# One-hot rows of the expert gates kept with two tokens side by side instead of eight

## The chip, the cores and the metric

The kernel runs on one core of a Trainium2 chip. The metric is the device time of one execution in microseconds (us). The engines are TensorE (PE; its weight loads are listed apart as PEld), VectorE (DVE), ScalarE (ACT), GpSimd (POOL) and SyncE (SP). Each runs its own stream of instructions in order and waits on semaphores for the others.

## What is computed

A decoder block on 1024 tokens: a mixing part (RWKV-7 and differential attention), and then an expert network, in which each token picks 128 of 16,384 experts by two keys, `e1` and `e2`, of 128 values each. Only the expert part matters here:

```python
ids = (e1 * PK_NKEYS + e2).reshape(T, PK_HEADS * PK_TOPK)
gates = jax.nn.softmax(vals, axis=-1).reshape(T, PK_HEADS * PK_TOPK)
act = jnp.einsum('ced,cd->ce', u_tab[idc], xc)
act = jax.nn.gelu(act, approximate=False) * gc
return jnp.einsum('ce,ced->cd', act, v_tab[idc])
```

## The kernel before

The tokens lie in eight tiles of 128. The experts of the first four tiles are gathered: `peer` fetches one row of `u` or `v` per token and step through POOL (L809) into one of five `uv` buffers, and DVE takes the dot product (L831) or adds the scaled row (L838). The last four tiles go through `dense`, which multiplies their tokens with all 16,384 experts on PE and weighs each product by a gate matrix that is mostly zero. `gates` builds that matrix ahead of `dense`, one block of 128 tokens at a time, four blocks in all; `choose` (the selection of the experts, on DVE) runs ahead of each block and `ahead` (some products `ua` for `dense`) beside it.

In `gates`, `e1`, `e2` and the gate `g` lie with the 128 picks of a token down the partitions and the tokens along the row. For four tokens, DVE writes `oh`, a float32 one-hot row of `e1` per pick (L850, four buffers). For eight tokens, DVE writes `ohb`, a bfloat16 one-hot row of `e2` (L854, two buffers), in the order [key value][token]: the eight tokens stand side by side, so that one token's 128 values are eight elements, or 16 bytes, apart. For each token ACT copies that row, scaled by `g`, to the float32 tile `ohg` (L859, two buffers of four tokens), and PE multiplies `ohg` with `oh` into a PSUM bank `gb` (L860). When four tokens are done ACT evicts the bank to `st` (L861), and every 32 tokens a store of 2 MB takes `st` to DRAM (`gd_s`, L862), from where `dense` reads it back.

The comparison pattern for `ohb` is a constant `eye8` of 1024 values, each key value eight times in a row. It comes from DRAM as float32 (`eye_f`, 512 KB, L960) and DVE casts it to bfloat16 (L962), while `pick` still ranks keys.

The order of instructions on each engine is fixed when the program is built, by a scheduler that weighs estimated costs; so `ohb`, `oh`, the steps of `choose` and the dot products L831 stand in one given order on DVE, whatever the times on the chip are. The stores and loads that are named here go through SP's queue, the gathers through POOL's.

Of the kernel before, what the change touches and what calls it, by code (L numbers as in the profile page):

```python
# [8 lines left out]
F32 = mybir.dt.float32  # L9
F32R = mybir.dt.float32r  # L10
BF = mybir.dt.bfloat16
I32 = mybir.dt.int32
U32 = mybir.dt.uint32
AF = mybir.ActivationFunctionType
OP = mybir.AluOpType
# [3 lines left out]
P = 128  # L19
# [29 lines left out]
def body(ctx: ExitStack, tc: tile.TileContext, ins, out, dbg=None):  # L49
    nc = tc.nc  # L50
# [15 lines left out]
    def abank(name):  # L66
        return ps.tile([P, 512], F32, name=name, tag="ab", bufs=2)
# [53 lines left out]
    def const(name, shape, dt=F32):  # L121
        t = kp.tile(shape, dt, name=name)
        nc.sync.dma_start(t, ins[name])
        return t
# [17 lines left out]
    eye_row = const("eye_row", [P, P])  # L142
# [680 lines left out]
    def peer(bi, ids, gate):  # L823

        rows = slice(bi * P, (bi + 1) * P)
        act = pp_.tile([P, P], F32, name="act", bufs=2)
        hb = pp_.tile([P, D], F32, name="hb", tag="ha", bufs=2)
        nc.sync.dma_start(hb, ins["hfs"][rows, :])
        for j in range(P):
            u = gather("u", ids, j)  # L830
            nc.vector.scalar_tensor_tensor(u, u, 1.0, hb, op0=OP.mult, op1=OP.mult, accum_out=act[:, j:j + 1])  # L831
        nc.scalar.activation(act, act, AF.Gelu)
        nc.vector.tensor_tensor(act, act, gate, op=OP.mult)
        acc = pp_.tile([P, D], F32, name="acc", tag="ha", bufs=2)
        nc.sync.dma_start(acc, ins["x1s"][rows, :])
        for j in range(P):
            v = gather("v", ids, j)
            nc.vector.scalar_tensor_tensor(acc, v, act[:, j:j + 1], acc, op0=OP.mult, op1=OP.add)  # L838
        finish(acc, rows, pp_, "uv", NU)

    def gates(sp, a, sl, eye8):

        e1, g = sl[:, 0:P], sl[:, 2 * P:3 * P]
        e2 = sl[:, 3 * P:].bitcast(BF)[:, 0:P]
        nc.scalar.activation(e2, sl[:, P:2 * P], AF.Copy)
        for q in range(0, P, QT):
            st = sp.tile([P, P, QT], F32, name="st", bufs=2)
            for t in range(0, QT, 4):
                o1 = sp.tile([P, 4, P], F32, name="oh", bufs=4)
                nc.vector.tensor_tensor(o1, eye_row[:, None, :].to_broadcast([P, 4, P]),  # L850
                                        e1[:, q + t:q + t + 4, None].to_broadcast([P, 4, P]), op=OP.is_equal)
                if t % 8 == 0:
                    o2 = sp.tile([P, P, 8], BF, name="ohb", bufs=2)
                    nc.vector.tensor_tensor(o2, eye8, e2[:, None, q + t:q + t + 8].to_broadcast([P, P, 8]),  # L854
                                            op=OP.is_equal)
                b = abank("gb")
                o3 = sp.tile([P, 4, P], F32, name="ohg", bufs=2)
                for k in range(4):
                    nc.scalar.activation(o3[:, k], o2[:, :, t % 8 + k], AF.Copy, scale=g[:, q + t + k:q + t + k + 1])  # L859
                    nc.tensor.matmul(b[:, k:512:4], o3[:, k], o1[:, k], start=True, stop=True)  # L860
                nc.scalar.activation(st[:, :, t:t + 4], b.rearrange("p (e t) -> p e t", t=4), AF.Copy)  # L861
            nc.sync.dma_start(ins["gd_s"][:, :, (a * P + q) // QT].rearrange("c p f t -> p c (f t)"),  # L862
                              st.rearrange("p (c f) t -> p c (f t)", f=CE))
# [6 lines left out]
    def ahead(sp, W, fh, fl, es):  # L870

        for e in es:
            t = sp.tile([P, 512], F32, name="ue", bufs=2)[:, :W]
            nc.scalar.activation(t, dots(e, W, fh, fl), AF.Copy)
            nc.sync.dma_start(ins["a_s"][e, :, 0:W], t)
# [80 lines left out]
        late = pick(t0, W, fh, fl)  # L956
    if "nopeer" not in dbg:
        with tc.tile_pool(name="sp", bufs=1) as sp:
            eye_f = sp.tile([P, P * 8], F32, name="eye_f", bufs=1)
            nc.sync.dma_start(eye_f, ins["eye8"])  # L960
            eye8 = sp.tile([P, P, 8], BF, name="eye8", bufs=1)
            nc.vector.tensor_copy(eye8.rearrange("p e t -> p (e t)"), eye_f)  # L962
            o = W - ND * P
            fh, fl = fh[:, :, o:W], fl[:, :, o:W]
            for a, c in enumerate(late[o // P:]):
                gates(sp, a, choose(*c), eye8)
                ahead(sp, ND * P, fh, fl, range(a * NE // ND, (a + 1) * NE // ND))
            todo += [(c[2], *choose(*c)) for c in late[:o // P]]
        dense(t0 + o, ND * P, fh, fl)
        for t in todo:  # L970
            peer(*t)


def prepare(inputs):
    import numpy as np
    g = {k: np.asarray(v) for k, v in inputs.items()}
    c = np.ascontiguousarray
    f = np.float32
    a = {}
    a["x"] = c(g["x"].reshape(T, D))  # L980

    wt = lambda w: c(w.reshape(2, 4, P, -1, P).transpose(3, 0, 2, 1, 4).reshape(-1, 2, P, 512))
    a["w_in"] = wt(g["w_in"][0])
    a["proj"] = wt(np.concatenate([g["proj_a"][0], g["proj_b"][0]], axis=0))
    a["w_out"] = c(g["w_out"][0].reshape(8, P, 2, 512).transpose(0, 2, 1, 3))
    a["wq"] = wt(g["peer_wq"][0])
    a["keysT"] = c(g["peer_keys"][0].reshape(16, P, P).transpose(0, 2, 1))
    a["u"], a["v"] = c(g["peer_u"][0]), c(g["peer_v"][0])
    a["ut"] = c(a["u"].reshape(P, P, 2, 4, P).transpose(0, 2, 4, 3, 1).reshape(P, 2, P, 512))
    a["nmw"] = c(g["norm_mix_w"][0].reshape(1, D))  # L990
    a["nfw"] = c(g["norm_ffn_w"][0].reshape(1, D))
    a["fnw"] = c(g["final_norm_w"].reshape(1, D))
    col = lambda v, n: v.reshape(n, P).T
    a["pp"] = c(np.concatenate(
        [col(g["shift_mu"][0], 14)]
        + [col(g[n][0].reshape(-1), 4) for n in ("w0", "a0", "k_k", "k_a", "r_k", "lnx_w", "lnx_b")]
        + [g["subln_w"][0].reshape(P, 1)], axis=1))
    a["lam4"] = c(np.stack([g["lam_q1"][0], g["lam_q2"][0], g["lam_k1"][0], g["lam_k2"][0]], axis=1))
    a["lora"] = c(np.stack([np.concatenate([g["w2"][0], g["a2"][0]], axis=0), g["g2"][0]], axis=1))

    a["ident"] = np.eye(P, dtype=f)
    s = np.arange(P)[:, None] % CH
    t = np.arange(CH)[None, :]
    a["mask2"] = c(np.concatenate([t > s, t >= s], axis=1).astype(f))
    lv = []
    for b in (16, 32):
        lv.append(((s // (2 * b)) == (t // (2 * b))) & ((t // b) % 2 == 1) & ((s // b) % 2 == 0))
    a["lvl"] = c(np.stack(lv, axis=1).astype(f))
    a["eyec"] = (s == t).astype(f)
    p = np.arange(P)  # L1010
    same = (p[:, None] // CH) == (p[None, :] // CH)
    a["eye16"] = c(np.tile(np.eye(16, dtype=f)[None], (64, 1, 1)))
    a["blk"] = same.astype(f)
    rm = np.ones((P, 512), f)
    rm[:, ::CH] = 0
    a["rmask"] = rm
    dq = np.arange(P)[:, None] - (np.arange(T)[None, :] - 896)
    a["dist"] = np.where(dq >= 0, -dq, NEG).astype(f)
    a["eye_row"] = c(np.tile(np.arange(P, dtype=f)[None], (P, 1)))
    a["eye8"] = c(np.tile(np.repeat(np.arange(P, dtype=f), 8)[None], (P, 1)))  # L1020
    a["iota"] = c(np.tile(np.repeat(np.arange(16, dtype=f), 16)[None], (P, 1)))
    return a

# [23 lines left out]
```

## Time and profile before

| | us |
|---|---|
| median of 3 runs | 3443.16 (3440.47 to 3446.24) |
| the profiled execution, its own time | 3435.12 |
| its span, first to last instruction | 3433.4 |
| PE busy | 3041.2 (89%) |
| DVE busy | 2855.4 (83%) |
| ACT busy | 1410.6 (41%) |
| POOL busy | 1328.8 (39%) |
| `ohg`, L859 on ACT, 512 instructions | 228.5 busy, 1.8 idle ahead of them |

The mixing part and the ranking of keys run to about 1549 us, the four gate blocks from there to about 1871 us, and `dense` beside the gathers from there to the end. A busy share is an average over these stages. In what follows a stage is read by itself: busy time of each engine within a stretch, and who waits for whom in it. The granted clock of PE is a share of its full speed.

### The profile page before, as it was taken

The page shows a single profiled execution, that of the slowest core. Times are in us where ns is not written, and L with a number is a line of the kernel's source. Part 1 is how long each engine was busy: PE and PEld are TensorE (multiplying, and loading weights), DVE is VectorE, ACT ScalarE, POOL GpSimd, SP SyncE. Part 2 cuts the span into 40 slices and gives each one's busy share as a digit, 9 for nine tenths or more (in the row PEclk, how much of TensorE's full clock was granted, in tenths as well). Part 3 has the DMA queues.
Part 4 walks back from the last instruction along what each step waited for, and adds up shares of the span by engine and source line. Part 5 has one row for each costly group of instructions (what it writes and reads, how often), then busy time and mean ns, then how long its engine had stood idle before and what let it go on. Part 6 is the DMA issues. An engine that isn't in the chain of part 4 may idle for free.

```text
span 3433.4 us, 50842 instructions
## 1 busy us (share of the span) xinstructions
PE 3041.2 (89%) x17382; PEld 2379.3 (69%) x17382; DVE 2855.4 (83%) x6337; ACT 1410.6 (41%) x2632; POOL 1328.8 (39%) x1037
## 2 busy tenths in 40 slices
PE   7999998989988878798887689999998999898992
PEld 5777777766766656576565568777777777676872
DVE  5565548989898789998887689998989999889997
ACT  4444424434434423239998333333323333333331
POOL 0000000054533454212124256655655665655664
PEclk9999999999999889899988799999999999999996
DMA  4222444276666788656769999999999999999997
GB/s 135 81 77 74 140 152 161 81 253 209 216 217 222 274 322 314 204 164 187 234 202 324 333 321 353 362 348 353 355 365 350 359 354 355 360 358 350 350 327 275
DMA packets 407525, 898.68 MB, mean 262 GB/s; under 512 B 69025, under 2 KB 140001, under 8 KB 403169
## 3 DMA queue, kind: packets, MB, share of 16 engines
q0 software_dynamic: 147456, 536.94, 43.8%
q1 hardware_dynamic: 259808, 358.49, 31.2%
q8 instruction: 137, 2.24, 0.3%
q14 instruction: 124, 1.01, 0.1%
HBM read 829.22 MB, written 66.07 MB: 261 GB/s over the span
## 4 chain that ended last, share of the span: by engine, by line
issue 30%; PE 23%; POOL 18%; DVE 13%; DMA 13%; ACT 2%; POOLq 0%; SPq 0%; DVEq 0%; ACTq 0%
POOL uv L809 18%; DMA uv<-v,ids 9%; PE z L192 3%; PE z L196 3%; PE z L193 3%; DVE acc L838 2%; DMA uv<-u,ids 2%; DVE uv L831 2%; PE sc L544 1%; ACT ohg L859 1%; DVE wlo L178 1%; PE q L192 1%; PE q L196 1%; PE q L193 1%; PE oT L586 1%
## 5 line engine op out<-in xcount | busy, mean ns | idle before, releaser
L809 POOL DMA_INDIRECT uv<-u,ids x512 | 652.6, 1275 | 1226.5 <-DVE uv L831 639.4
L809 POOL DMA_INDIRECT uv<-v,ids x512 | 674.1, 1317 | 519.7 <-DVE acc L838 329.1
L838 DVE SCALAR_TENSOR_TENSOR acc<-uv,act,acc 128x1024 f32<-128x1024 f32 x512 | 655.9, 1281 | 75.7 <-DMA uv<-v,ids 70.1
L831 DVE SCALAR_TENSOR_TENSOR uv<-uv,hb 128x1024 f32<-128x1024 f32 x512 | 617.1, 1219 | 92.9 <-DMA uv<-u,ids 91.9
L177 ACT ACTIVATE whi<-wraw 128x512 fp32r<-128x512 f32 x552 | 339.8, 628 | 611.4 <-PE z L193 201.3
L178 DVE TENSOR_TENSOR wlo<-wraw,whi 128x512 fp32r<-128x512 f32 x552 | 375.0, 686 | 117.3 <-ACT whi L177 95.8
L192 PE MATMUL ua<-fh,whi 128*128 128x512 f32 x1024 | 415.9, 406 | 52.6 <-ACT ye L921 28.6
L193 PE MATMUL ua<-fl,whi 128*128 128x512 f32 x1024 | 413.3, 404 | 0.0
L199 ACT ACTIVATE ah<-gw 128x512 fp32r<-128x512 f32 x128 | 80.9, 632 | 682.4 <-DVE gw L901 682.4
L203 PE MATMUL yk<-vh,ah 128*128 128x512 f32 x768 | 308.5, 402 | 24.4 <-ACT ah L199 22.4
L205 PE MATMUL yk<-vh,al 128*128 128x512 f32 x768 | 308.4, 402 | 7.0 <-DVE al L200 6.7
L204 PE MATMUL yk<-vl,ah 128*128 128x512 f32 x768 | 304.3, 396 | 8.7 <-DVE vl L200 8.6
L196 PE MATMUL z<-hh,wlo 128*128 128x512 f32 x672 | 276.7, 412 | 6.0 <-DVE wlo L178 6.0
L192 PE MATMUL z<-hh,whi 128*128 128x512 f32 x672 | 276.6, 412 | 4.0 <-DVE carry L287 3.8
L196 PE MATMUL ua<-fh,wlo 128*128 128x512 f32 x1024 | 266.3, 398 | 15.3 <-DVE wlo L178 15.1
L193 PE MATMUL z<-hl,whi 128*128 128x512 f32 x672 | 274.6, 409 | 0.0
L192 PEld LDWEIGHTS ua<-fh,whi 128*128 128x128 f32 x1024 | 199.9, 195 | 100.2 <-ACT ye L921 32.1
L860 PE MATMUL gb<-oh,ohg 128*128 128x128 f32 x1024 | 226.4, 341 | 41.3 <-ACT ohg L859 40.4
L860 PEld LDWEIGHTS gb<-oh,ohg 128*128 128x128 f32 x1024 | 165.9, 209 | 105.2 <-ACT ohg L859 69.5
L196 PEld LDWEIGHTS ua<-fh,wlo 128*128 128x128 f32 x1024 | 193.1, 191 | 61.2 <-DVE wlo L178 22.3
L193 PEld LDWEIGHTS ua<-fl,whi 128*128 128x128 f32 x1024 | 200.0, 195 | 42.3
L859 ACT ACTIVATE ohg<-ohb,sl 128x128 f32<-128x128 bf16 x512 | 228.5, 538 | 1.8 <-DVE ohb L854 1.8
(322 smaller groups left out, 5644.7 us busy)
## 6 DMA issues: line engine op xcount, KB each, us to landing
wraw<-ut SPq DMA_DIRECT2D x256, 256.0 KB, 6.6
vraw<-v SPq DMA_DIRECT2D x256, 256.0 KB, 6.4
wraw<-w_in SPq DMA_DIRECT2D x168, 256.0 KB, 2.8
gd_s<-st SPq DMA_DIRECT2D x16, 2048.0 KB, 11.9
gt<-gd_s SPq DMA_DIRECT2D x32, 1024.0 KB, 8.9
wraw<-wq SPq DMA_DIRECT2D x64, 256.0 KB, 2.9
g_s<-sgo SPq DMA_DIRECT2D x32, 256.0 KB, 3.7
wraw<-proj SPq DMA_DIRECT2D x32, 256.0 KB, 4.1
```

Source lines behind the costliest of these rows:

```text
L177: nc.scalar.activation(hi, raw, AF.Copy)
L178: nc.vector.tensor_tensor(lo, raw, hi.bitcast(F32), op=OP.subtract)
L192: nc.tensor.matmul(o, hi, xh(k), start=(k == 0), stop=False)
L193: nc.tensor.matmul(o, hi, xl(k), start=False, stop=False)
L196: nc.tensor.matmul(o, lo, xh(k), start=False, stop=(k == n - 1))
L203: nc.tensor.matmul(o, ah, bh, start=first, stop=False)
L204: nc.tensor.matmul(o, ah, bl, start=False, stop=False)
L205: nc.tensor.matmul(o, al, bh, start=False, stop=last)
L809: nc.gpsimd.indirect_dma_start(out=t, out_offset=None, in_=ins[src], in_offset=bass.IndirectOffsetOnAxis(ap=ids[:, j:j + 1], axis=0))
L831: nc.vector.scalar_tensor_tensor(u, u, 1.0, hb, op0=OP.mult, op1=OP.mult, accum_out=act[:, j:j + 1])
L838: nc.vector.scalar_tensor_tensor(acc, v, act[:, j:j + 1], acc, op0=OP.mult, op1=OP.add)
L860: nc.tensor.matmul(b[:, k:512:4], o3[:, k], o1[:, k], start=True, stop=True)
```

## The change

The one-hot rows `ohb` take the order [pair of tokens][key value][token of the pair]. One token's 128 values are then two elements, or 4 bytes, apart. The DVE instruction that writes them compares the same 1024 bfloat16 values, with a pattern of four dimensions: the constant `eye2` (each key value twice, 256 values) is repeated over the four pairs, and the pair of `e2` values is repeated over the key values. ACT reads the new place. `eye2` is cast by DVE from `eye_row`, a tile that is loaded at the start of the program; `eye_f`, its load and the array `eye8` are gone.

```diff
-    def gates(sp, a, sl, eye8):
+    def gates(sp, a, sl, eye2):
...
-                    o2 = sp.tile([P, P, 8], BF, name="ohb", bufs=2)
-                    nc.vector.tensor_tensor(o2, eye8, e2[:, None, q + t:q + t + 8].to_broadcast([P, P, 8]),
-                                            op=OP.is_equal)
+                    o2 = sp.tile([P, 4, P, 2], BF, name="ohb", bufs=2)
+                    nc.vector.tensor_tensor(o2, eye2[:, None].to_broadcast([P, 4, P, 2]),
+                                            e2[:, q + t:q + t + 8].rearrange("p (a b) -> p a b", b=2)[:, :, None, :]
+                                            .to_broadcast([P, 4, P, 2]), op=OP.is_equal)
...
-                    nc.scalar.activation(o3[:, k], o2[:, :, t % 8 + k], AF.Copy, scale=g[:, q + t + k:q + t + k + 1])
+                    nc.scalar.activation(o3[:, k], o2[:, (t % 8 + k) // 2, :, k % 2], AF.Copy, scale=g[:, q + t + k:q + t + k + 1])
...
-            eye_f = sp.tile([P, P * 8], F32, name="eye_f", bufs=1)
-            nc.sync.dma_start(eye_f, ins["eye8"])
-            eye8 = sp.tile([P, P, 8], BF, name="eye8", bufs=1)
-            nc.vector.tensor_copy(eye8.rearrange("p e t -> p (e t)"), eye_f)
+            eye2 = sp.tile([P, P, 2], BF, name="eye2", bufs=1)
+            nc.vector.tensor_copy(eye2, eye_row[:, :, None].to_broadcast([P, P, 2]))
...
-                gates(sp, a, choose(*c), eye8)
+                gates(sp, a, choose(*c), eye2)
...
-    a["eye8"] = c(np.tile(np.repeat(np.arange(P, dtype=f), 8)[None], (P, 1)))
```

The new lines move the line numbers: L859 of before is L861 of the change, L860 is L862 and L861 is L863. On ACT, here where the first gate block begins, the order of before is:

```order
729 L798 ACTIVATE sl<-sl 128x384
730 L781 ACTIVATE te<-ch 128x2048
731 L845 ACTIVATE sl<-sl 128x128
732 L859 ACTIVATE ohg<-ohb,sl 128x128 x7
733 L861 ACTIVATE st<-gb 128x128x4
734 L859 ACTIVATE ohg<-ohb,sl 128x128 x3
735 L861 ACTIVATE st<-gb 128x128x4
```

Of the change, at the same place of ACT:

```order
729 L798 ACTIVATE sl<-sl 128x384
730 L781 ACTIVATE te<-ch 128x2048
731 L845 ACTIVATE sl<-sl 128x128
732 L861 ACTIVATE ohg<-ohb,sl 128x128 x7
733 L863 ACTIVATE st<-gb 128x128x4
734 L861 ACTIVATE ohg<-ohb,sl 128x128 x3
735 L863 ACTIVATE st<-gb 128x128x4
```

Nothing moves here: but for line numbers, ACT's whole order stays as it was.

On DVE, at the beginning of the ranking of the last four tiles, the difference between before (-) and the change (+) is:

```order
 L838 SCALAR_TENSOR_TENSOR acc<-uv,act,acc 128x1024
 L249 TENSOR_TENSOR fl<-tr,fh 128x4x128 x2
+L962 CAST eye_14187<-eye_row 128x256
 L838 SCALAR_TENSOR_TENSOR acc<-uv,act,acc 128x1024 x2
 L178 TENSOR_TENSOR wlo<-wraw,whi 128x512
-L962 CAST eye_14189<-eye_f 128x1024
 L838 SCALAR_TENSOR_TENSOR acc<-uv,act,acc 128x1024 x2
```

The cast moves three instructions ahead, shrinks to a quarter and reads a tile that is there from the start. Elsewhere on DVE the end of the first gathered tile (`finish`, L820) moves from inside the first gate block to the last steps of the ranking, a dot product L831 takes its old place, and some neighbours within `choose` change places. POOL's order stays.

On SP, at the same time of the program, the difference begins so:

```order
 L686 DMA x1s<-x_12591 128x1024
 L686 DMA x1s<-x_12593 128x1024
-L117 DMA wraw<-wq 128x512 x3
-L960 DMA eye_f<-eye 128x1024
+L117 DMA wraw<-wq 128x512 x5
+L704 DMA keyt<-keysT 128x128
+L117 DMA wraw<-wq 128x512 x2
```

The load of `eye_f` is gone, and the loads of `wq` close up. The stores and loads of L820's tile move ahead of the first `gd_s` stores with it.

## Rows read from the trace of the kernel before

**Rows 1.** Windows by stage: length, busy us (count) per engine, PE clock, DMA share, GB/s.

```profile
1397.00:1549.00 152.00, 142.70 (x647) 112.09 (x647) 146.84 (x697) 53.75 (x87) 22.08 (x21) 0.96 0.52 166
1549.00:1871.00 322.00, 272.33 (x1229) 200.65 (x1228) 267.12 (x630) 303.36 (x682) 78.29 (x66) 0.90 0.74 232
2500.00:3000.00 500.00, 468.21 (x1976) 376.80 (x1977) 459.89 (x640) 164.14 (x297) 300.76 (x232) 0.97 0.97 357
```

**Rows 2.** The same by gate block, then the passage to `dense`: PE, PEld, DVE, ACT, POOL.

```profile
1552.70:1631.50 78.80, 65.88 (x295) 47.35 (x295) 67.16 (x176) 76.44 (x171) 17.38 (x13) 0.91 0.67 203
1631.50:1712.00 80.50, 68.04 (x315) 49.44 (x314) 68.65 (x182) 76.61 (x172) 17.07 (x14) 0.94 0.73 230
1712.00:1791.00 79.00, 66.01 (x298) 50.12 (x297) 61.60 (x158) 73.00 (x166) 16.55 (x15) 0.85 0.62 186
1791.00:1870.50 79.50, 68.20 (x306) 50.26 (x305) 65.83 (x110) 74.30 (x170) 26.80 (x24) 0.91 0.97 318
1870.50:1905.00 34.50, 17.27 (x63) 13.36 (x61) 18.39 (x31) 5.95 (x10) 13.62 (x12) 0.74 0.92 321
```

**Rows 3.** The tile `ohg`: L859's durations (min/median/max ns); who waited for its users.

```profile
L859 ACT ACTIVATE ohg<-ohb,sl x512: 502/520/679, 1552.7 to 1868.7; 128x128 f32<-128x128 bf16 x171
...
  PE gb L860: 40.4, 97
  DVE oh L850: 29.1, 45
  DVE ohb L854: 13.6, 20
```

**Rows 4.** ACT's order in time: start us, us (of a merged run), instruction, count.

```profile
1591.92 0.58 ACT L861 ACTIVATE st<-gb 128x512 f32<-128x512 f32 x1
1592.39 1.76 ACT L859 ACTIVATE ohg<-ohb,sl 128x128 f32<-128x128 bf16 x4
1594.06 0.59 ACT L861 ACTIVATE st<-gb 128x512 f32<-128x512 f32 x1
```

**Rows 5.** L566 on ACT, float32 side by side: its durations; one pair in time.

```profile
L566 ACT ACTIVATE dg<-ident,sm x32: 384/394/425, 751.2 to 1167.9; 128x128 f32<-128x128 f32 x32
...
920.17 0.68 ACT L566 ACTIVATE dg<-ident,sm 128x128 f32<-128x128 f32 x2
```

**Rows 6.** PE in time: products L860 with nothing to wait for, then L192.

```profile
1633.80 0.83 PE L860 MATMUL gb<-oh,ohg 128*128 128x128 f32 x6
1634.38 0.48 PE L192 MATMUL ua<-fh,whi 128*128 128x512 f32 x1
```

**Rows 7.** Groups on DVE: shapes, count, busy us, mean ns, idle ahead.

```profile
L831 DVE SCALAR_TENSOR_TENSOR uv<-uv,hb 128x1024 f32<-128x1024 f32 x512 | 617.1, 1219 | 92.9 <-DMA uv<-u,ids 91.9
...
L850 DVE TENSOR_TENSOR oh<-eye_row,sl 128x512 f32<-128x512 f32 x128 | 87.4, 690 | 31.0 <-PE gb L860 29.1 <-ACT sl L798 1.1
...
L854 DVE TENSOR_TENSOR ohb<-eye,sl 128x1024 bf16<-128x1024 bf16 x64 | 43.8, 688 | 13.8 <-ACT ohg L859 13.6
...
L776 DVE CAST ch<-d 128x256 bf16<-128x256 f32 x8 | 2.3, 289 | 0.0
```

**Rows 8.** DVE in time around the constant's cast; the idle time ahead in brackets.

```profile
1401.51 0.69 DVE L178 TENSOR_TENSOR wlo<-wraw,whi 128x512 fp32r<-128x512 f32 x1 [0.45 <-ACT whi L177]
1405.07 0.69 DVE L962 CAST eye<-eye_f 128x1024 bf16<-128x1024 f32 x1 [2.87 <-DMA eye_f<-eye]
1405.68 1.28 DVE L838 SCALAR_TENSOR_TENSOR acc<-uv,act,acc 128x1024 f32<-128x1024 f32 x1
```

**Rows 9.** DVE's waits in the third block: us in total, times, longest.

```profile
DVE wlo L178 <- ACT whi L177: 3.9, 2, 2.6
```

**Rows 10.** Waits from 1872 to 1920 us.

```profile
PE yk L203 <- ACT ah L199: 17.3, 1, 17.3
ACT whi L177 <- DMA wraw<-ut: 13.8, 1, 13.8
```

## Prediction

> **What bounds the kernel now.** I read the windows by stage first, because the busy shares of the whole span hide this place: ACT is busy 41% of the span but 303.36 of the 322 us of the gate stage [rows 1]. Cut by block it is plainer: in the four blocks ACT is busy 76.44, 76.61, 73.00 and 74.30 us, 300.35 of 317.8 us together, against 263.24 for DVE and 268.13 for PE [rows 2]. Next come the waits. PE stood 40.4 us waiting for `ohg`, DVE 29.1 us until PE gave back `oh` and 13.6 us until ACT gave back `ohb` [rows 3]: both stand behind ACT. Then ACT's order in time: one cycle of four tokens goes from 1591.92 to 1594.06, 2.14 us, made of one eviction and four `ohg` copies without a gap [rows 4]. So the gate stage is bound by ACT, and three quarters of it is one instruction, L859.
>
> PE's 268 us are not work of that length. A busy PE instruction includes its wait in the pipe. Where nothing held it, six L860 instructions took 1634.38 - 1633.80 = 0.58 us [rows 6], about 0.1 us each, 0.8 us of PE in a cycle of 2.14 us. PE is not next in line; DVE is.
>
> **ACT's copies.** L859 has a median of 520 ns for 128 elements that lie 16 bytes apart [rows 3]. The nearest row with a step of 4 bytes is L566: also 128 elements, also a scale by a column, and 394 ns, in float32 side by side [rows 5]. Four L859 take 1.76 us in a row, so each starts (1.76 - 0.52) / 3 = 0.41 us behind the last [rows 4]; two L566 take 0.68 us, so 0.68 - 0.394 = 0.286 us [rows 5]. The new copy reads bfloat16 every 4 bytes, a form that no row shows. The bounds are 0.286 us (only the distance in bytes counts) and 0.41 us (it doesn't count). I take 0.286 us, since the two rows are alike in length, scale and output and differ in step and type of the input. That takes 512 x 0.124 = 63.5 us off ACT: 300.35 becomes 237 us.
>
> The Trainium skill has two pages that part ways here. "Advanced Engine Details and Errata", Memory Cachelines, says that SBUF is read in lines of 16 bytes and needs at least two hits on a line for full speed: by it eight-token rows miss on every element and two-token rows hit four times, which is what L859 and L566 show. "ScalarE: Activation LUTs", What ACT_TABLE_LOAD costs, gives an instruction's time by its length and pointers alone, one element per cycle, with no word on steps: an estimate by it is 186 + 0.833 x 128 + 93 = 386 ns for L859, which the measured 520 contradicts and the measured 394 of L566 meets.
>
> **What is late then.** With ACT at 237 us DVE's 263.24 us come last, in an order that doesn't change here. DVE's own idle time in the blocks is 317.8 - 263.24 = 54.6 us [rows 2]. Where DVE is the bound it still isn't gapless: 146.84 of 152 us, 96.6%, in the ranking stage [rows 1]. 263.24 / 0.966 = 272.5 us. A wait of 3.9 us for a weight tile in the third block comes from a load, not from L859, and stays [rows 9]. The last block moves 318 GB/s at a DMA share of 0.97 [rows 2], and the steady stage reaches 357 [rows 1]: it can't be shorter than 79.5 x 318 / 357 = 70.8 us, 2.7 more than 65.83 / 0.966 = 68.1. That makes 279 us at best. At worst half of today's idle time stays, as hand-offs between DVE, ACT and PE: 263.2 + 27.3 = 290.5 us. Two buffers of `ohb` and four of `oh` let DVE run ahead, and ACT is then loaded 237 / 285 = 83%; I take the middle, 285 us: **33 us saved**.
>
> **The one-hot write on DVE.** L854 handles 1024 bfloat16 in 688 ns, L850 only 512 float32 in 690, so L854 runs at two elements per step; 1024 float32 in L831 take 1219 ns [rows 7]. The new write has the same count and type, but runs of two instead of eight in one operand. Bounds: 688 ns, and 1219 ns if the double rate is lost. I take 688: two neighbours still stand side by side in all operands. On this the Trainium skill ("Advanced Engine Details and Errata", 2x-1p Requirements) asks for 16-bit types, a unit step in the innermost dimension and a start at a multiple of four bytes, and the new pattern keeps all three.
>
> **The constant.** Before, DVE stands 2.87 us for `eye_f` and casts for 0.69 us [rows 8]; the new cast has 256 values, 0.289 us by L776 [rows 7], and waits for nothing. DVE is the bound there, so at most 2.87 + 0.69 - 0.29 = 3.3 us; nothing, if the next gather (L838 stands right behind) isn't there yet either. I take 2 us. The 512 KB load that goes frees the queue for a moment; no engine but DVE waited for it.
>
> **What stays.** The move of L820, its store and its loads is a swap with one dot product on a DVE that does both anyway: 0. The passage of 34.5 us to `dense` hangs on loads: ACT waits 13.8 us for `wraw`, PE 17.3 us for `ah` [rows 10]; I leave it. `dense` with its gathers runs with DMA at 0.97 and PE and DVE above 90% [rows 1], in an unchanged order, so it starts and ends earlier by the same amount. The gathers can't be left behind: their buffers are freed by DVE's dot products, which come earlier too, and the stage has room for them at 0.62 to 0.73 in three blocks [rows 2].
>
> **Sum.** 3435.1 (the profiled execution's own time) - 33 - 2 = 3400. The median of the runs stands 8 us above that execution, so the forecast for the median is 3443.2 - 35 = **3408 us**.
>
> **Rivals.**
> 1. ACT gives the time back to others: in the first three blocks half of DVE's idle time of 11.6 + 11.9 + 17.4 = 40.9 us stays, the last block, at a DMA share of 0.97, gains nothing, and the constant's wait turns into one for the gather. Saved 20 us: 3423. For it speaks the tight mesh of three in-order engines; against it that most of DVE's waits name ACT or PE behind ACT.
> 2. The step isn't the cost; L859 stays at 520 ns because of its type. Only the constant is won: 3441. For it speaks that no row has bfloat16 read by a copy of this length. Against it, the eviction of 512 elements takes 0.58 us [rows 4], hardly more than a copy of 128: something in L859 is charged per element. By the "ScalarE: Activation LUTs" rule of the Trainium skill the step would not matter, and this rival would hold.
> 3. Slower: runs of two break the double rate on DVE, which is now the bound. At 1219 ns the 64 writes cost 64 x 0.531 / 0.966 = 35 us, the blocks take 285 + 35 = 320, and the total is 3443, no change. It is slower by over 0.2% (6.9 us) from about 1.32 us per write: (317.8 + 2 + 6.9 - 285) x 0.966 / 64 = 0.63 us above 0.688. If a broken run cost DVE what the wide step costs ACT, (520 - 394) / 128 = 1 ns per element on top, a write would take 2.2 us: 64 x 1.53 / 0.966 = 101, total 3510. The middle of the slower stretch is 3477. Only runs of eight are in the trace; for it speaks no row, against it only that pairs stay together.
>
> **How the numbers follow.** Forecast 0.67, from 3393 (DVE at 96.6% with no further wait, and the whole of the constant: 48.6 us, rounded out) to 3422; rival 1 0.16, faster; rival 2 0.07, within 0.2%, which is about what a measurement of this kernel can tell from no change; rival 3 0.10, of it 0.04 at no change and 0.06 slower. Faster 0.83, same 0.11, slower 0.06. The range of 3393 to 3438 leaves out rivals 2 and 3 and a little below.
>
> **What the profile would show.** L861 (the old L859) at a median near 394 ns and a cycle of four tokens near 1.65 us where DVE doesn't hold it; ACT idle ahead of it, waiting for `ohb` on DVE, instead of 1.8 us; DVE's idle time in the blocks down from 54.6 us to some 22; L854 still at 688 ns; no wait at the cast; the blocks 285 us together and the passage still near 34. I'm wrong if L861 stays at 520, if `ohb` takes over 1.2 us, or if the blocks shrink and the passage or `dense` grows by as much.

## The result and the profile after

The changed kernel takes 3400.86 us (median; 3389.99 to 3414.72), against 3444.7 us before in the same comparison. The ratio is 0.9879, with a 95% interval of 0.985 to 0.9908: 32 to 52 us less. The forecast was 35 us less and 3408 us.

The profiled execution of the change took 3406.55 us, its span 3404.8. The gate blocks, from the first copy to `ohg` to the last eviction, went from 317.2 to 278.1 us. The windows by block answer to [rows 2] (length, then busy time and count of PE, PEld, DVE, ACT, POOL, PE clock, DMA share, GB/s):

```profile
1565.50:1633.30 67.80, 52.54 (x294) 43.91 (x293) 65.17 (x176) 62.92 (x170) 16.36 (x13) 0.94 0.73 226
1633.30:1704.90 71.60, 57.18 (x318) 47.95 (x317) 67.43 (x182) 64.31 (x173) 16.88 (x14) 0.96 0.80 249
1704.90:1780.30 75.40, 60.57 (x333) 51.23 (x332) 67.29 (x172) 62.94 (x173) 19.01 (x15) 0.95 0.74 230
1780.30:1843.60 63.30, 47.72 (x269) 40.77 (x267) 54.57 (x91) 56.74 (x162) 25.36 (x22) 0.95 1.00 341
```

ACT's 300 us are now 246.9, DVE's 263 are 254.5, and DVE has become the busier of the two, idle for 23.6 us in place of 54.6. The tile `ohg` shows why (durations as min/median/max ns; then who waited for its users, in us and times), against [rows 3]:

```profile
L861 ACT ACTIVATE ohg<-ohb,sl x512: 386/389/403, 1565.5 to 1842.7; 128x128 f32<-128x128 bf16 x171
...
  PE gb L862: 46.2, 98
  DVE oh L850: 8.0, 10
  ACT st L863: 6.2, 8
  DVE ohb L855: 5.0, 5
```

The copy fell from 520 to 389 ns. DVE's waits for `oh` and `ohb` fell from 42.7 to 13.0 us; PE's wait for `ohg` did not fall. In ACT's order in time (start, us, instruction, count) a cycle of four tokens is still without a gap, as in [rows 4], but shorter:

```profile
1590.89 0.60 ACT L863 ACTIVATE st<-gb 128x512 f32<-128x512 f32 x1
1591.38 1.26 ACT L861 ACTIVATE ohg<-ohb,sl 128x128 f32<-128x128 bf16 x4
1592.64 0.60 ACT L863 ACTIVATE st<-gb 128x512 f32<-128x512 f32 x1
```

1592.64 - 1590.89 = 1.75 us, against 2.14. The groups on DVE (count, busy us, mean ns, idle ahead) answer to [rows 7, 8]: the new write costs no more than the old, and the cast waits for nothing.

```profile
L855 DVE TENSOR_TENSOR ohb<-eye,sl 128x1024 bf16<-128x1024 bf16 x64 | 43.4, 682 | 5.2 <-ACT ohg L861 5.0
...
L962 DVE CAST eye<-eye_row 128x256 bf16<-128x256 f32 x1 | 0.3, 283 | 0.0
```

By stage, in us (mixing ends with the last store of `x1s`, `dense` begins with its first GELU on ACT, so that the passage is counted some 10 us further than in [rows 2]; the last column is a second profile of the change, from the first experiment):

| stage | before | after | after again |
|---|---|---|---|
| mixing | 1364.9 | 1382.6 | 1373.0 |
| ranking, first `choose` | 187.8 | 182.9 | 185.1 |
| gate blocks | 317.2 | 278.1 | 273.9 |
| passage to `dense` | 44.8 | 48.5 | 46.2 |
| `dense` and gathers | 1518.7 | 1512.7 | 1516.4 |
| span | 3433.4 | 3404.8 | 3394.6 |

Two things ask for an experiment. The mixing part, whose instructions the change doesn't touch, took 17.7 us longer. And the constant, ACT's copies and the load that is gone came together.

### The profile page after: what moved, and what is told of

Same layout as the page of the kernel before. It is cut to its first block, busy times and chain, and to the rows that moved or that the text cites. A ratio compares the mean times of both kernels' runs of the same rounds, so it can differ in the third digit from the quotient of the medians.

```text
span 3404.8 us, 50837 instructions
## 1 busy us (share of the span) xinstructions
PE 2999.7 (88%) x17382; PEld 2368.9 (70%) x17382; DVE 2849.4 (84%) x6337; ACT 1356.1 (40%) x2632; POOL 1305.0 (38%) x1037
## 4 chain that ended last, share of the span: by engine, by line
issue 32%; PE 25%; POOL 18%; DMA 12%; DVE 12%; ACT 1%; POOLq 0%; SPq 0%; DVEq 0%; ACTq 0%
POOL uv L809 18%; DMA uv<-v,ids 8%; PE z L192 3%; PE z L196 3%; PE z L193 3%; DMA uv<-u,ids 2%; DVE acc L838 2%; DVE uv L831 1%; PE sc L544 1%; DVE wlo L178 1%; PE q L192 1%; PE q L196 1%; PE q L193 1%; PE pT L578 1%; PE oT L586 1%
## 5 line engine op out<-in xcount | busy, mean ns | idle before, releaser
L809 POOL DMA_INDIRECT uv<-v,ids x512 | 653.3, 1276 | 530.1 <-DVE acc L838 343.9
L831 DVE SCALAR_TENSOR_TENSOR uv<-uv,hb 128x1024 f32<-128x1024 f32 x512 | 617.0, 1217 | 98.4 <-DMA uv<-u,ids 97.4
L192 PE MATMUL ua<-fh,whi 128*128 128x512 f32 x1024 | 415.5, 406 | 51.6 <-ACT ye L923 26.1
L192 PE MATMUL z<-hh,whi 128*128 128x512 f32 x672 | 278.2, 414 | 4.0 <-DVE carry L287 3.8
L192 PEld LDWEIGHTS ua<-fh,whi 128*128 128x128 f32 x1024 | 199.8, 195 | 98.9 <-ACT ye L923 29.1
L862 PE MATMUL gb<-oh,ohg 128*128 128x128 f32 x1024 | 176.3, 313 | 46.5 <-ACT ohg L861 46.2
L862 PEld LDWEIGHTS gb<-oh,ohg 128*128 128x128 f32 x1024 | 154.0, 194 | 72.6 <-ACT ohg L861 69.7
L203 PEld LDWEIGHTS yk<-vh,ah 128*128 128x128 f32 x768 | 147.2, 192 | 62.9 <-ACT ah L199 29.8
```

Of the source, the lines that this page charges most:

```text
L192: nc.tensor.matmul(o, hi, xh(k), start=(k == 0), stop=False)
L203: nc.tensor.matmul(o, ah, bh, start=first, stop=False)
L809: nc.gpsimd.indirect_dma_start(out=t, out_offset=None, in_=ins[src], in_offset=bass.IndirectOffsetOnAxis(ap=ids[:, j:j + 1], axis=0))
```

## The experiments

Ratios are to the kernel before in the same comparison, with 95% intervals; stages are those of the table.

**The change again.** No edit.

> The changed kernel once more, with a second profile. In the first profile its mixing part, whose instructions are the same in both kernels, took 17.7 us longer than before (last store of x1s at 1382.6 against 1364.9 us), and all the rest 46 us less. Theory: that is scatter from one execution to the next, so here the mixing part ends anywhere between 1355 and 1385 us, while the gate blocks take 278 us again (within 4) and the total is 0.985 to 0.991 of before. Rival: the change itself lengthens the mixing part (another place of the tensors in DRAM); then it ends near 1382 again.

Measured: 0.9872 (0.9847 to 0.9897), 3398.3 us. The gate blocks took 273.9 us, a hair more below 278 than was allowed for. The mixing part ended at 1373.0 us. The stores of `x1s` in four profiles (after the durations stand the start of the first store and of the last one): before, after, the change again, and the run below whose rows of eight lie 32 bytes apart:

```profile
L686 SPq DMA_DIRECT2D x1s<-x x8: 319/323/327, 521.0 to 1364.9; - x8
```

```profile
L686 SPq DMA_DIRECT2D x1s<-x x8: 319/323/326, 522.0 to 1382.6; - x8
```

```profile
L686 SPq DMA_DIRECT2D x1s<-x x8: 319/323/327, 520.8 to 1373.0; - x8
```

```profile
L686 SPq DMA_DIRECT2D x1s<-x x8: 319/323/327, 521.6 to 1396.5; - x8
```

All agree to 1.2 us at the first store and then spread over 32 us, and the latest has the old layout. The place of the tensors in DRAM doesn't explain it either: the run with the constant alone, from whose DRAM `eye8` is gone as in the change, ended mixing at 1366.9 us. So it is scatter of the stretch between these stores, and the profile of before is the earliest of all fourteen; what in the stretch scatters was not tested. Totals of single executions can't be compared to better than some 15 us here; the later stages can.

**The layout alone.** The old constant is still loaded and cast, beside the new one:

```diff
+            eye_f = sp.tile([P, P * 8], F32, name="eye_f", bufs=1)
+            nc.sync.dma_start(eye_f, ins["eye8"])
+            eye8 = sp.tile([P, P, 8], BF, name="eye8", bufs=1)
+            nc.vector.tensor_copy(eye8.rearrange("p e t -> p (e t)"), eye_f)
             eye2 = sp.tile([P, P, 2], BF, name="eye2", bufs=1)
```

> Two-token rows, but the 512 KB load of the old constant and its cast of 1024 values stay (the cast's output is not read; the two-token pattern is cast from the small tile beside it). Theory: the gain is ACT's copies; the gate blocks take 278 us as in the change, DVE again waits some 2.9 us for the load in the ranking stage, and the total is 3 to 5 us above the change, about 3406 us. Rival: the load that is gone matters more than its wait; then the total loses 10 us or more against the change.

Measured: 0.9897 (0.9867 to 0.9927), 3405.26 us; gate blocks 274.9 us. The copies take as long as in the change, and DVE waits for the load (start, us, idle time ahead in brackets):

```profile
L861 ACT ACTIVATE ohg<-ohb,sl x512: 384/390/403, 1558.3 to 1832.2; 128x128 f32<-128x128 bf16 x171
```

```profile
1409.18 0.70 DVE L964 CAST eye<-eye_f 128x1024 bf16<-128x1024 f32 x1 [4.29 <-DMA eye_f<-eye]
```

The ranking up to the last load of `keyt` takes 137.7 us, against 133.1 in the change again: 4.6 us, the 4.29 us of wait among them. The total is 7 us above the change again, where 3 to 5 were expected; the intervals allow both.

**The constant alone.** Rows of eight, but:

```diff
-            nc.vector.tensor_copy(eye8.rearrange("p e t -> p (e t)"), eye_f)
+            nc.vector.tensor_copy(eye8, eye_row[:, :, None].to_broadcast([P, P, 8]))
```

with the load gone.

> Eight-token rows as before, but the constant is cast from the small tile and the 512 KB load is gone. Theory: the copies on ACT stay at 520 ns, the gate blocks take 318 us, the ranking stage is 3 us shorter; total 3 to 5 us below before, about 3440 us, 0.9985 to 0.999. Rival: the load that is gone is worth 10 us or more.

Measured: 0.9992 (0.9975 to 1.0009), 3438.62 us: the total alone can't be told from no change. Its gate blocks took 316.2 us, its copies a median of 524 ns, and its ranking up to the last load of `keyt` 132.9 us against 136.1 before.

```profile
L859 ACT ACTIVATE ohg<-ohb,sl x512: 502/524/628, 1551.5 to 1866.2; 128x128 f32<-128x128 bf16 x171
```

The load is worth about its wait; nearly all of the change's gain is ACT's copies.

**Four side by side, and 32 bytes apart.** One run takes rows of four (8 bytes), the other rows of eight in a tile padded to sixteen (32 bytes), the constant from the small tile:

```diff
-                    o2 = sp.tile([P, 4, P, 2], BF, name="ohb", bufs=2)
+                    o2 = sp.tile([P, 2, P, 4], BF, name="ohb", bufs=2)
...
```

```diff
-                    o2 = sp.tile([P, P, 8], BF, name="ohb", bufs=2)
-                    nc.vector.tensor_tensor(o2, eye8, e2[:, None, q + t:q + t + 8].to_broadcast([P, P, 8]),
+                    o2 = sp.tile([P, P, 16], BF, name="ohb", bufs=2)
+                    nc.vector.tensor_tensor(o2[:, :, 0:8], eye8, e2[:, None, q + t:q + t + 8].to_broadcast([P, P, 8]),
...
```

> Four tokens side by side: one token's values are 8 bytes apart. By the rule of the Trainium skill (Advanced Engine Details and Errata, Memory Cachelines) two reads fall on each 16-byte line and that is enough: the copy takes 390 ns as at 4 bytes, and the gate blocks 278 us. Rival, a cost that grows with the step: 8 bytes lie between 389 and 520 ns, near 430, so each copy starts 0.04 us later, 512 x 0.04 = 20 us of ACT, and the blocks take 290 us or more.

> Eight-token rows in a tile padded to sixteen: one token's values lie 32 bytes apart, the constant is cast from the small tile. If every read that opens a new line pays the same (the rule of the Trainium skill, Advanced Engine Details and Errata, Memory Cachelines), the copy stays at 520 ns and the gate stage at 316 us, total about 3440. If the cost goes on growing with the distance, the copy takes over 600 ns, and the stage 316 + 40 us or more.

Measured at 8 bytes, then at 32 (tile `ohb`, the copy's row):

```profile
L861 ACT ACTIVATE ohg<-ohb,sl x512: 388/398/416, 1554.7 to 1830.2; 128x128 f32<-128x128 bf16 x171
```

```profile
L859 ACT ACTIVATE ohg<-ohb,sl x512: 505/522/648, 1581.7 to 1901.9; 128x128 f32<-128x128 bf16 x171
```

With 389 ns at 4 bytes and 520 at 16 this is a step, not a slope: nearly flat up to 8 bytes, and the same at 16 and 32. The gate blocks follow, 276.5 and 321.6 us; the totals are 0.9854 (0.9819 to 0.989) and 1.0007 (0.9989 to 1.0025). The Trainium skill ("Advanced Engine Details and Errata", Memory Cachelines) puts the edge between two reads of a 16-byte line and one, and that is where it lies in these runs; the rising cost that was the rival falls.

**One token by itself.** The values lie 2 bytes apart, and DVE's write repeats the token's value in its innermost place:

```diff
-                    o2 = sp.tile([P, 4, P, 2], BF, name="ohb", bufs=2)
+                    o2 = sp.tile([P, 8, P], BF, name="ohb", bufs=2)
...
+                                            e2[:, q + t:q + t + 8, None].to_broadcast([P, 8, P]), op=OP.is_equal)
```

> One token by itself: its 128 values stand side by side, 2 bytes apart, and in exchange the token's value is repeated with step 0 in the innermost place of DVE's write. Theory of rival 3's price: DVE loses the double rate, the write takes 1.22 us instead of 0.68, 64 x 0.54 = 34 us more of DVE, and since DVE and ACT are now nearly level the gate blocks grow by 25 to 40 us against the change, so the total is 3425 to 3445 us. If DVE is not near the bound, the blocks stay at 278 us. The copy on ACT takes 390 ns as at 4 bytes.

Measured: 1.0013 (0.9992 to 1.0034), 3455.59 us. The copy and the write (tile `ohb`):

```profile
L860 ACT ACTIVATE ohg<-ohb,sl x512: 385/390/402, 1566.7 to 1839.4; 128x128 f32<-128x128 bf16 x171
L855 DVE TENSOR_TENSOR ohb<-eye,sl x64: 1197/1218/1226, 1565.4 to 1833.4; 128x1024 bf16<-128x1024 bf16 x64
```

The price of the write, 1218 ns, is rival 3's within a nanosecond, and the total is its "no change". The place is not. The gate blocks stayed at 273.7 us, and `dense` took 1578.9 us, 62 more than in the change again. With the dearer write the scheduler's order holds fewer dot products in the stage: on DVE 35 of them lie between the first one-hot write and the last, against 61 in the change, and 707 instructions on gathered rows lie behind the start of `dense`, against 679. So this run does not test what DVE bounds; it asks what a gather costs later.

**Less DVE, less ACT.** Both leave out work: every second write of `oh`, or the fourth of four copies to `ohg`.

```diff
+                if t % 8 == 0:
+                    o1 = sp.tile([P, 4, P], F32, name="oh", bufs=4)
...
```

```diff
-                    nc.scalar.activation(o3[:, k], o2[:, (t % 8 + k) // 2, :, k % 2], AF.Copy, scale=g[:, q + t + k:q + t + k + 1])
...
+                    if k < 3:
+                        nc.scalar.activation(o3[:, k], o2[:, (t % 8 + k) // 2, :, k % 2], AF.Copy, scale=g[:, q + t + k:q + t + k + 1])
...
```

> Leaves out work: every second one-hot write of e1 on DVE (L850), its predecessor being used again; 64 x 0.61 = 39 us less of DVE in the gate blocks. If DVE is the bound there (the prediction's reading), the blocks fall from 278 to 245 or so. If ACT's cycle of 1.755 us for four tokens is the bound, in which ACT has no gap, they stay within 8 us of 278, since 128 x 1.755 = 225 us and ACT's other work of some 25 us stay.

> Leaves out work: of four copies to ohg on ACT the fourth, the third being used twice; 128 x 0.29 = 37 us less of ACT. If DVE is the bound, the blocks stay within 8 us of 278 (DVE was busy 254.5 us of them). If ACT's cycle is the bound, they fall by 20 us or more. If both this and the run with fewer writes on DVE change little, the two engines are level and each holds the other.

Measured: with fewer writes 0.9781 (0.9741 to 0.982), gate blocks 290.3 us; with fewer copies 0.9922 (0.9888 to 0.9955), gate blocks 234.8 us. Both miss what was expected, and the total goes the other way than the blocks: the longer blocks give the faster kernel. The scheduler moved the dot products again: 94 of them lie in the gate stage in one, 29 in the other, against 61. So neither run tests one engine alone. With fewer writes DVE was as busy in the blocks as in the change (254.6 us) and ACT too (246.2 us); what grew is DVE's wait for gathered rows, here before, in the change and with fewer writes (us, times, longest):

```profile
DVE uv L831 <- DMA uv<-u,ids: 3.4, 5, 1.2
```

```profile
DVE uv L831 <- DMA uv<-u,ids: 7.3, 10, 1.4
```

```profile
DVE uv L831 <- DMA uv<-u,ids: 19.0, 27, 1.8
```

For the total the work left behind the start of `dense` decides. The gathers in `dense` (window, length, POOL's busy time and count, PE clock, DMA share, GB/s) in the change again, with one token by itself, with fewer writes and with fewer copies:

```profile
1878.20:3394.60 1516.40, 869.76 (x674) 0.96 0.94 346
```

```profile
1876.00:3454.90 1578.90, 899.45 (x704) 0.94 0.94 343
```

```profile
1906.60:3371.10 1464.50, 820.04 (x640) 0.97 0.94 347
```

```profile
1843.30:3423.50 1580.20, 901.24 (x711) 0.94 0.94 345
```

From 640 to 704 gathers `dense` grows by 114.4 us, 1.8 us for each on average, at nearly the same rate in GB/s; from 704 to 711 it hardly grows, so the price of one isn't fixed. Its matrix products are the same in all four, 5760 on PE.

**Fewer gathers.** Leaves out the last 32 gathers of `v` of one tile, with their additions; the order stays otherwise.

```diff
-        for j in range(P):
+        for j in range(P - 32 if bi == 3 else P):
             v = gather("v", ids, j)
```

> Leaves out work: the last 32 of the 128 gathers of v, with their additions, for one gathered tile; in all 647 gathers stand behind the start of dense in DVE's order instead of 679. If dense ends when the gathers end, at 2.2 us per gather that is left (1513 us for 675 in the changed kernel), the total falls by 50 to 70 us. If the matrix products of dense (PE above 90%) set its end, it falls by 10 us at most.

Measured: 0.9752 (0.9724 to 0.9779), 3362.24 us; gate blocks 278.0 us, as in the change.

```profile
1890.70:3361.70 1471.00, 831.35 (x644) 0.97 0.95 346
```

`dense` is 45 us shorter than in the change again for 30 gathers less in it, 1.5 us each. The fall is a little under the 50 to 70 us that were expected and far over 10: the stream of gathers sets the end here, not the products. 1.5 us is also what one gather's 128 x 4 KB take at 346 GB/s; DVE's addition for it, 1.28 us, was left out with it, so DMA and DVE aren't told apart by this.

**A slower write of e1, order kept.** Every second `oh` reads its pattern at a step of 16 bytes. The gate stage holds 61 dot products, as in the change:

```diff
+                row = eye4[:, :, 0] if t % 8 == 0 else eye_row
-                nc.vector.tensor_tensor(o1, eye_row[:, None, :].to_broadcast([P, 4, P]),
+                nc.vector.tensor_tensor(o1, row[:, None, :].to_broadcast([P, 4, P]),
```

> DVE's one-hot writes of e1 read their pattern every 16 bytes in every second instruction; the count of gathers in the gate stage (60 in DVE's order, 61 in the change) stays. If a wide step costs DVE what it costs ACT, 1 ns per element, these 64 writes take 1.2 us instead of 0.69, 33 us more of DVE. If DVE bounds the gate stage together with ACT, the stage grows from 274 to 278 us to 295 or more; if ACT alone does, DVE's idle time of some 20 us takes most of it and it stays below 290. If the writes still take 0.69 us, DVE doesn't feel the step, and the run only says that.

Measured: 0.9914 (0.9881 to 0.9947). The two kinds of write (groups on DVE), and the gate blocks in a window:

```profile
L851 DVE TENSOR_TENSOR oh<-eye,sl 128x512 f32<-128x512 f32 x64 | 68.6, 1071 | 5.5 <-PE gb L863 5.1 <-ACT sl L798 0.4
L851 DVE TENSOR_TENSOR oh<-eye_row,sl 128x512 f32<-128x512 f32 x64 | 43.7, 683 | 0.8 <-PE gb L863 0.8
```

```profile
1571.80:1861.10 289.30, 222.39 (x1205) 185.51 (x1205) 275.89 (x618) 247.16 (x675) 90.08 (x63) 0.93 0.80 253
```

The write cost 25 us more on DVE, where 33 were expected, and the blocks became 11 to 15 us longer (289.3 against 278.1 and 273.9), just under the 290 up to which ACT alone was to be the bound. Some 10 us vanished in DVE's idle time and the rest came through. ACT's wait for `ohb`, in the change and then here (us, times, longest), rose with it:

```profile
ACT ohg L861 <- DVE ohb L855: 1.8, 2, 1.2
```

```profile
ACT ohg L862 <- DVE ohb L856: 7.6, 10, 1.9
```

So ACT alone doesn't bound the stage of the change, and DVE's added work came through only in part. That the two are about level is the reading that fits; no run changed one of them by enough, at the same order, to measure it.

**Two tries at a better kernel.** Wider writes save DVE fixed parts: rows of `e1` for eight tokens and of `e2` for sixteen, or the latter alone.

```diff
-                if t % 8 == 0:
+                if t % 16 == 0:
...
-                    o2 = sp.tile([P, 4, P, 2], BF, name="ohb", bufs=2)
+                    o2 = sp.tile([P, 8, P, 2], BF, name="ohb", bufs=2)
...
```

> A try at a better kernel: DVE writes the one-hot rows of e1 for eight tokens at a time (two buffers instead of four) and those of e2 for sixteen, which saves 64 + 32 instructions with a fixed part of some 0.15 us each (0.69 us for 512 values, 1.22 for 1024), 14 us of DVE. If DVE is the bound the blocks fall to 265 to 270 us; if ACT's cycle is, they stay at 278; if the coarser hand-over costs more, they grow.

> A try at a better kernel: DVE writes the two-token rows for sixteen tokens at a time, 32 instructions instead of 64, each of 1.22 us. In its order DVE then has 66 gathers' work in the gate stage instead of 61 and 675 behind the start of dense instead of 679. By 2.2 us per gather dense is 9 us shorter; the gate stage takes 5 more dot products (6 us) and saves 32 fixed parts (5 us). Total 8 us below the change, 0.985 of before; if the coarser hand-over to ACT costs as much, no gain.

Measured: 0.9879 (0.9844 to 0.9914) and 0.9887 (0.9866 to 0.9908): no gain over the change. The gate blocks took 290.9 and 289.0 us. `dense` with 672 gathers took 1519.0 and 1510.2 us. What the wide writes were to save is lost in the stage, which takes more dot products (68 and 66, against 61) and hands over in coarser pieces. The waits differ: with both widened DVE's wait for PE ahead of `oh` rose from 8.0 to 16.7 us, with rows of sixteen alone its wait for gathered rows from 7.3 to 14.1. Which of the two costs more was not tried.

## Why the prediction was right, step by step

**The total: 44 us less, where 35 were forecast.** The blocks, 39 and 43 us shorter in the two profiles, and the ranking, some 3 us shorter, make up the 44. The 9 us beyond the forecast are nearly all the blocks, which were forecast at 285 us.

**What bounded the kernel: right.** ACT's copies bounded the gate stage. With the constant alone the blocks stayed at 316.2 us, with the layout alone they fell to 274.9.

**The price of a copy: right, 389 ns for 394.** The doubt whether bfloat16 at 4 bytes would read like float32 side by side is settled by the steps: 4 and 8 bytes alike, 16 and 32 alike. Rival 2 falls.

**ACT's load after: too low, 247 us for 237.** The copies themselves fell by 228.5 - 162.0 = 66.5 us of busy time. But the copies no longer overlap with the eviction behind them. Before, the eviction started 0.09 us ahead of the end of the copies (1594.06, against 1592.39 + 1.76 [rows 4]); now it starts exactly at their end (1592.64). It is so in general: over the 124 places where an eviction follows a copy, the two overlap by a median of 0.10 us before and by under 0.01 us in both profiles of the change. That makes the cycle 1.75 us instead of the 1.65 that the prediction named, 0.1 x 128 = 13 us in all, which covers the 10. That the eviction waits there for PE's products, which it follows more closely than before, is likely (ACT's waits for PE ahead of evictions rose from 1.0 to 6.2 us) but was not tested.

**DVE next: half right.** DVE's idle time fell to 23.6 and 19.4 us, against the 22 that the 285 us held. That 22 was the middle between two bounds, so the agreement is partly luck: 7.3 us of it are waits for gathered rows, up from 3.4 before, which the prediction put at nothing ("the stage has room for them"). And DVE did not become the bound by itself. The sign that was named for it, ACT idle ahead of its copies until DVE has written `ohb`, did not come: 1.8 us as before. The cycle shown runs without a gap on ACT, and of the slower write of `e1` about half came through.

**285 us for the blocks: 278 and 274 measured.** Two terms were too long. DVE's 263.24 us were taken as work that stays, but fell to 254.5. Some 3 us of it left the stage: the instructions of L820, whose move the prediction had put at 0, and by time one dot product. Most of the rest is overlap. An instruction right behind another starts some 0.08 us before the end of it, one after a wait doesn't; with fewer waits 581 and 582 of 616 instructions in the two profiles start so, against 526 of 619 before. The single durations sum to 299.9 us before and to 295.0 and 298.4 in the change. And the floor of 70.8 us for the last block was wrong: it took 63.3 us. Bytes per block aren't fixed: 341 GB/s x 63.3 us is 21.6 MB where 318 x 79.5 was 25.3. The third block moved 2.6 MB more than before (230 x 75.4 against 186 x 79.0), and the passage, which grew by 1.4 to 3.7 us, 1.6 MB more (340 x 48.5 against 332 x 44.8). So rival 1 falls, though its first half was near: it gave the first three blocks 20 us, and they became 23.5 us shorter, but the last one, which it gave nothing, became 16.2 us shorter.

**The constant: 2 us forecast, 3 to 5 measured** in the ranking (136.1 to 133.3, 133.1 and 132.9; 137.7 with the load back).

**What stays: right, by a reason that was only half stated.** `dense` took 1512.7 and 1516.4 us, against 1518.7. The prediction said that it starts and ends earlier by the same amount because the order stays. The runs show what in the order mattered: the gathers left behind the start of `dense`, 676 before, 675 and 674 after. With 704 a gate stage as short as the change's gave nothing in the total (one token by itself); with 640 a longer gate stage gave a faster kernel (fewer writes).

**Rival 3: its price right, its way wrong.** Runs of two keep the double rate, 682 ns. A write at 1218 ns did bring the total back to before, not by a longer gate stage but by gathers pushed into `dense`.

## What to carry to other kernels

Where an engine is the bound in one stage only, look at the bytes between neighbouring elements that it reads; here two reads per 16 bytes were enough, and one made each element dearer. Before a saved stage is booked, ask what the end of the kernel hangs on: count how much of that work the scheduler's order leaves for the end, before and after. Here the gain arrived because that count stayed the same. Where executions scatter by more than an edit is worth, compare stages that begin and end with named instructions.

## What the runs showed of the hardware

- A copy of 128 bfloat16 on ACT took 390 ns at a step of 2 bytes, 389 at 4, 398 at 8, 520 at 16 and 522 at 32; so some 1 ns per element more at 16 bytes, and no more than that at 32.
- DVE feels such a step too: 512 float32 compared with one operand at 16 bytes took 1071 ns instead of 683, 0.76 ns per element more.
- DVE's double rate for 16-bit data held with runs of two in one operand (682 ns for 1024 values) and was lost when the innermost place of that operand had step 0 (1218 ns).
